# The same instructions on other SBUF addresses: all matmul operands of a two-layer decoder trunk at 128 modulo 512 bytes

## The chip, the cores and the metric

The kernel runs on one core of a Trainium2 chip. The metric is the time of one execution on the device in microseconds; the median of three runs of the kernel before is 2660.34 us (2660.19 to 2660.78). A profile of one further execution is used beside it. A core has TensorE (PE, matrix products, with the weight loads PEld), VectorE (DVE), ScalarE (ACT), GpSimd (POOL) and SyncE (SP, which issues most DMAs). SBUF is the memory that TensorE reads its two operands from: the stationary one, loaded ahead as weights, and the moving one, streamed through. An SBUF tile has 128 partitions and lies at the same byte address in each of them. "At 128" below is short for a byte address that leaves 128 when divided by 512.

## The reference, cut to what matters

Two residual layers over x of 1024 rows and 1024 columns, float32. The first mixes tokens with a gated spatial product in chunks of 128, the second with dilated windowed attention in three patterns; each is followed by a squared-ReLU MLP of width 4096.

```python
for i in range(DEPTH):                       # 2
    shift, scale, gate = ada_mod(c, ada_w[i, 0], ada_b[i, 0])
    h = x * (1.0 + scale) + shift
    y = mixer_a(h, ...) if i % 2 == 0 else mixer_b(h, ...)
    x = layer_norm(ALPHA * x + gate * y, ln_g[i, 0], ln_b[i, 0])
    shift, scale, gate = ada_mod(c, ada_w[i, 1], ada_b[i, 1])
    h = x * (1.0 + scale) + shift
    y = squared_relu_mlp(h, mlp_w_up[i], mlp_w_down[i])
    x = layer_norm(ALPHA * x + gate * y, ln_g[i, 1], ln_b[i, 1])
```

## The kernel before, in words

Nearly all the time goes into matmuls of 128 x 128 weights against 128 x 512 moving columns, in a float32 format of reduced precision. To keep float32 accuracy every operand is cut into a high part (a cast on ScalarE, L113) and a low part (a subtraction on VectorE, L114), and every product takes three matmuls: high by high, high by low, low by high. The names show it: `lhi`, `llo` are the parts of a left operand, `rhi`, `rlo` those of a right one. In a row of the profile `psd<-rhi,lhi` the tile written in PSUM stands first, then the moving operand, then the stationary one.

The stages, in order of time:

- mixer A, about 50 to 330 us: a projection (L530), the spatial product (L415), a second projection (L776), transposes with the identity (L791) and the output projection (L434).
- the MLP of layer 1 (j=1): the up-projection (L989) with seven block products in place of eight, then the down-projection (L1156), again seven products of 192 matmuls each, about 647 to 956 us.
- the projections to q, k and v of attention in blocks (L1500), to about 1330 us.
- attention, about 1375 to 1970 us: for eight pairs of heads and three dilations the scores (L1694, q against k), a softmax, transposes of the probabilities p with the identity (L1747, L1750), the split of the transposed probabilities (`pThi`, `pTlo`), and the product with v (L1774). Between these narrow matmuls of 64 to 256 columns stand the projections of the next q and k (L1601), 512 columns each, three to a step of the contraction, and then the start of the output projection (L1978). The bands of dilation 1 read q and k in blocks from DRAM (`bq`, `bk`).
- the rest of the output projection (L1978), whose weight unit 7 (`wo`) stands in a buffer of the tag `v`, and the MLP of layer 2 (j=3): L989 to about 2340 us, L1156 from about 2350 us to the end.

The modulation vectors (`ada`) are formed in the background: weights are summed by VectorE, split into `adahi` and `adalo`, and summed over partitions by two matmuls against `ones_r` (L161, L162), twenty times in all.

Where a tile lies is decided by pools. A pool takes the next free bytes when it is opened, on the left side upwards, on the right side downwards from the top, and holds one region for each tag. `cst` (constants) and `small` (statistics) stand first on the left; so their sizes shift all that follows. `edge` is a tile on the right that nothing reads: its size alone shifts all pools on the right side. `lead` and `pad` are such tiles on the left.

The order of instructions is written out by hand or kept by the recording layer, engine by engine; a tile's address has no part in it.

The down-projection uses, for its split operands, fourteen places in turn (`split_tile`, L1083): eight in `wts` and six in the pool `split1` or `split3` that the phase opens. In layer 2 that pool stands 128 bytes further than in layer 1, since the statistics of the last row tile (`st4`, L339) take 128 bytes in the pool below it.

Of the kernel before, what the change touches and what calls it, by code (L numbers as in the profile page):

```python
# [10 lines left out]
F32 = mybir.dt.float32  # L11
F32R = mybir.dt.float32r
AF = mybir.ActivationFunctionType
ALU = mybir.AluOpType
# [3 lines left out]
P = 128  # L18
# [11 lines left out]
EPS = 1e-5  # L30
# [5 lines left out]
def trunk(ctx: ExitStack, tc: tile.TileContext, x, c, ada_w, ada_b, ln_g, ln_b, a_w_in, a_b_in,  # L36
# [4 lines left out]
    V, A, G, T = nc.vector, nc.scalar, nc.gpsimd, nc.tensor  # L41

    def pool(stack, name, bufs, **kw):
        return stack.enter_context(tc.tile_pool(name=name, bufs=bufs, reuse_waits="tile", **kw))

    cst = pool(ctx, "cst", 1)
    small = pool(ctx, "small", 4)
    small.tile([P, 16], F32, name="pad", bufs=1)
    edge = pool(ctx, "edge", 1, side="right")
    edge.tile([P, 24], F32, name="edge")  # L50
    act = pool(ctx, "act", 4)
    wts = pool(ctx, "wts", 4)
    work = pool(ctx, "work", 2)
# [3 lines left out]
    y_out = out.rearrange("b s d -> (b s) d")  # L57


    eps = cst.tile([P, 1], F32, name="eps")  # L60
    V.memset(eps[:], EPS)
    cst.tile([P, 24], F32, name="lead")
    ident = cst.tile([P, P], F32, name="ident")
    make_identity(nc, ident[:])
    ones_r = cst.tile([P, P], F32R, name="ones_r")
# [5 lines left out]
    cols_b = cols_c[:, KD : KD + 64]  # L71
    silu_c = cst.tile([P, KD], F32, name="silu_c")
    one = cst.tile([P, 1], F32, name="one")
    with ExitStack() as first:
        tmp = pool(first, "tmp", 1)
        ps0 = pool(first, "ps0", 1, space=PSUM)
        rows_c = tmp.tile([P, P], F32, name="rows_c")
        V.memset(rows_c[:], 0.0)
        nc.sync.dma_start(rows_c[0:KD, :], c.rearrange("b (k p) -> (b k) p", p=P))
        ones = tmp.tile([P, P], F32, name="ones")  # L80
        V.memset(ones[:], 1.0)
        V.tensor_copy(ones_r[:], ones[:])
        V.memset(one[:], 1.0)
        ptc = ps0.tile([P, P], F32, name="rows_ct")
        T.transpose(ptc[:], rows_c[:], ident[:])
        V.tensor_copy(cols_c[:, 0:KD], ptc[:, 0:KD])
        sg = tmp.tile([P, KD], F32, name="sg")
        A.activation(sg[:], cols_c[:, 0:KD], AF.Sigmoid)
        V.tensor_tensor(silu_c[:], cols_c[:, 0:KD], sg[:], op=ALU.mult)

    def g_col(j):
        return cols[:, o_g + j * KD : o_g + (j + 1) * KD]

    def b_col(j):
        return cols[:, o_b + j * KD : o_b + (j + 1) * KD]
# [7 lines left out]
    def bank(kind, name):  # L103
        return ps[kind].tile([P, HALF], F32, name=name, tag=kind)
# [6 lines left out]
    def split(hi, lo, src, hi_engine=A, lo_engine=V):  # L111

        first = A.copy(hi, src) if hi_engine is A else hi_engine.tensor_copy(hi, src)  # L113
        return first, lo_engine.tensor_tensor(lo, src, hi, op=ALU.subtract)  # L114


    ada = [dict() for _ in range(4)]
# [4 lines left out]
    def ada_steps(j, order, raw_bufs=2):  # L122


        i, s = divmod(j, 2)
        todo = []
        for part, h in order:
            box = {}
            w0 = part * D + h * HALF

            def step(k, part=part, h=h, box=box, w0=w0):
                nm = f"{j}_{part}_{h}"
                raw = ada_p.tile([P, HALF], F32, name=f"adaw_{nm}_{k}", tag="adaw", bufs=raw_bufs)
                nc.sync.dma_start(raw[:], ada_w[i, s, k * P : (k + 1) * P, w0 : w0 + HALF])
                if k == 0:
                    acc = box["acc"] = ada_p.tile([P, HALF], F32, name=f"adaacc_{nm}", tag=f"adaacc{part % 2}")
                    ins = V.tensor_scalar(acc[:], raw[:], silu_c[:, 0:1], None, ALU.mult)
                else:
                    acc = box["acc"]
                    ins = V.scalar_tensor_tensor(acc[:], raw[:], silu_c[:, k : k + 1], acc[:], ALU.mult, ALU.add)  # L140
                tc.keep_in_program_order(ins)

            def bias_row(part=part, h=h, box=box, w0=w0):
                if part == 2:
                    row = box["row"] = ada_p.tile([P, HALF], F32, name=f"adab_{j}_{h}", tag="adaw", bufs=raw_bufs)
                    nc.sync.dma_start(row[0:1, :], ada_b[i, s, w0 : w0 + HALF].unsqueeze(0))

            def reduce(part=part, h=h, box=box):
                nm = f"{j}_{part}_{h}"
                acc = box["acc"]  # L150
                hi, lo = (ada_p.tile([P, HALF], F32R, name=f"ada{m}_{nm}", tag=f"ada{m}") for m in ("hi", "lo"))
                if part == 2:
                    V.tensor_tensor(acc[0:1, :], acc[0:1, :], box["row"][0:1, :], op=ALU.add)
                split(hi[:], lo[:], acc[:])
                box["sum"] = (hi, lo)

            def total(part=part, h=h, box=box, w0=w0):
                nm = f"{j}_{part}_{h}"
                hi, lo = box["sum"]
                pst = bank("tr", f"psa_{nm}")  # L160
                T.matmul(pst[:], ones_r[:], hi[:], start=True, stop=False)  # L161
                T.matmul(pst[:], ones_r[:], lo[:], start=False, stop=True)  # L162
                row = ada_p.tile([P, HALF], F32, name=f"gaterow_{nm}", tag="gaterow")
                if part == 2:
                    V.tensor_scalar(row[:], pst[:], 1.0, None, ALU.add)
                    nc.sync.dma_start(gate_dram[j, w0 - 2 * D : w0 - 2 * D + HALF].unsqueeze(0), row[0:1, :])
                    return
                A.copy(row[:], pst[:])
                nc.sync.dma_start(mod_dram[j, part, h * HALF : (h + 1) * HALF].unsqueeze(0), row[0:1, :])

            def fetch(part=part, h=h):
                if part < 2:
                    ada[j][part, h] = cst.tile([P, 4], F32, name=f"ada_{j}_{part}_{h}")
                    nc.sync.dma_start(ada[j][part, h][:], mod_dram[j, part, h * HALF : (h + 1) * HALF].rearrange("(k p) -> p k", p=P))

            def columns(part=part, h=h):
                if part == 2:
                    return
                bias = cols_b[:, 16 * j + 8 * part + 4 * h : 16 * j + 8 * part + 4 * h + 4]
                res = ada[j][part, h][:]  # L180
                V.scalar_tensor_tensor(res, res, float(part), bias, ALU.add, ALU.add)
                if part == 0:
                    sh, sc = ada[j][0, h], ada[j][1, h]
                    mul = cst.tile([P, 4], F32, name=f"mul_{j}_{h}")
                    add = cst.tile([P, 4], F32, name=f"add_{j}_{h}")
                    o = slice(4 * h, 4 * h + 4)
                    V.tensor_tensor(mul[:], g_col(j - 1)[:, o], sc[:], op=ALU.mult)
                    V.tensor_tensor(add[:], b_col(j - 1)[:, o], sc[:], op=ALU.mult)
                    V.tensor_tensor(add[:], add[:], sh[:], op=ALU.add)
                    ada[j]["mul", h], ada[j]["add", h] = mul, add  # L190

            steps = [lambda k=k, step=step: step(k) for k in range(KD)]
            todo.append((steps[:-1] + [bias_row, steps[-1], reduce] if part == 2 else steps + [reduce], (total, fetch, columns)))
        return todo

# [91 lines left out]
    class Residual:  # L287
# [48 lines left out]

        def stats_in_quarters(self, i, quarters):
            if i not in self.st:
                self.st[i] = vec.tile([P, 32], F32, name=f"st_{self.j}_{i}", tag="st4")[:, 0:24].rearrange("p (q n) -> p q n", n=6)  # L339
            for q in quarters:  # L340
                V.bn_stats(self.st[i][:, q, :], self.acc[i][:, q * 256 : (q + 1) * 256])

# [1172 lines left out]
    def attention(form):  # L1515
# [5 lines left out]
        with ExitStack() as ph:  # L1521
            open_psum(ph, "B", sc=2, pv=2, mm=2, tr=2)
            ql = pool(ph, "attn_qlo", 1)
            vec = pool(ph, "vecB", 1)
            qk = {g: pool(ph, f"attn_qk{g}", 1, side="right") for g in (1, 2)}
            qp = pool(ph, "attn", 2)

            near = ql.tile([P, 2 * P], F32, name="near")
            G.iota(near[:], pattern=[[-1, 2 * P]], base=P, channel_multiplier=1, allow_small_or_imprecise_dtypes=True)
# [491 lines left out]
            lead, credit = 7 * KD, 0  # L2021
# [27 lines left out]
    ahead = values_ahead(right)  # L2049
    done = mlp(1, done, ahead)  # L2050
    done, go_on = attention(values(done, right, ahead))
    with ExitStack() as ph:
        open_psum(ph, "C", mm=8)
# [27 lines left out]
```

## Time and profile before

| | |
|---|---|
| median of 3 runs | 2660.34 us |
| the profiled execution | 2658.99 us |
| its span | 2657.3 us |
| instructions in the span | 36921 |
| matmuls on TensorE | 13144 |
| HBM read and written | 365.95 MB and 136.95 MB, 189 GB/s over the span |
| DMA queue of SP | 444.22 MB, 52.5% of 16 engines' span |
| L1156, down-projections, high by high | 344.6 us busy, 880 matmuls, mean 392 ns |
| L989, up-projections, `psua` | 363.1 us busy, 1536 matmuls, mean 390 ns |

A row of the view by line gives line, engine, operation, tiles, shapes and count, then busy microseconds and the mean duration of one in ns, then the idle time of the engine just before, with what ended it. The duration of a matmul is counted from its start to its last result; matmuls overlap, so the distance between two starts is shorter than the duration. The view of one line gives the smallest, the median and the largest duration, and the starts of the first and the last.

### The profile page before, as it was taken

To read this page: it belongs to the slowest core of one execution; us is meant where nothing else is said; L and a number is where in the kernel's file an instruction comes from. 1 tells how busy PE (TensorE), PEld (TensorE's weight loads), DVE (VectorE), ACT (ScalarE), POOL (GpSimd) and SP (SyncE) were. 2 spreads that over 40 slices of the span, in tenths; PEclk is the share of its full clock that TensorE was granted. 3 is DMA by queue.
4 is the path that set the end of the run, shared out by engine and by line. 5 is a ranking of instruction groups with operands and counts; after the bars stand their busy time and mean duration, and the time that the engine had idled before them with its cause. 6 is when DMAs were issued, how large, how long until landed. Compare 5 with 4: busy or idle time off the path is not lost.

```text
span 2657.3 us, 36921 instructions
## 1 busy us (share of the span) xinstructions
PE 2636.0 (99%) x13144; PEld 2178.5 (82%) x13144; DVE 1979.1 (74%) x3558; ACT 1397.0 (53%) x2639; POOL 104.8 (4%) x190
## 2 busy tenths in 40 slices
PE   8999999999999999999999999999999999999998
PEld 6888888888888888888888888888888888888887
DVE  6886898886988787655557777777668965677877
ACT  5454576555444554333446666666657655554432
POOL 0000000000000001111110000000010000000000
PEclk9999999999999999999999999999999999999999
DMA  8543367778867546555565554455783654495562
GB/s 298 186 122 117 129 200 238 238 232 286 315 213 248 184 151 231 196 199 198 176 183 159 151 158 133 133 136 157 238 205 118 225 185 147 157 311 186 182 205 81
DMA packets 341554, 505.35 MB, mean 190 GB/s; under 512 B 58092, under 2 KB 175444, under 8 KB 341368
## 3 DMA queue, kind: packets, MB, share of 16 engines
q1 hardware_dynamic: 324936, 444.22, 52.5%
q0 software_dynamic: 16432, 58.76, 6.2%
q8 instruction: 103, 1.69, 0.3%
q14 instruction: 83, 0.68, 0.1%
HBM read 365.95 MB, written 136.95 MB: 189 GB/s over the span
## 4 chain that ended last, share of the span: by engine, by line
PE 94%; DVE 3%; DMA 2%; ACT 1%; issue 0%; SPq 0%; POOL 0%; DVEq 0%; ACTq 0%; POOLq 0%
PE psd L1156 23%; PE psua L989 13%; PE psv L1500 13%; PE psk L1601 7%; PE psq L1601 7%; PE psuc L989 7%; PE psd_wout L434 3%; PE psu L776 3%; PE psub L989 3%; PE pv L1774 3%; PE sc L1694 3%; PE psv L530 3%; PE pT L1747 1%; PE psoa L1978 1%; PE psoe L1978 1%; PE psod L1978 1%
## 5 line engine op out<-in xcount | busy, mean ns | idle before, releaser
L989 PE MATMUL psua<-right,left 128*128 128x512 f32 x1536 | 363.1, 390 | 0.1
L1156 PE MATMUL psd<-rhi,lhi 128*128 128x512 f32 x880 | 344.6, 392 | 0.0
L1156 PE MATMUL psd<-rhi,llo 128*128 128x512 f32 x880 | 343.3, 390 | 0.0
L1156 PE MATMUL psd<-rlo,lhi 128*128 128x512 f32 x880 | 342.3, 389 | 0.0
L989 PEld LDWEIGHTS psua<-right,left 128*128 128x128 f32 x1536 | 287.2, 188 | 61.7 <-DVE right L114 0.6
L1716 ACT ACTIVATE p<-p,stat 128x128 f32<-128x128 f32 (+1 forms) x384 | 168.8, 441 | 96.0 <-DVE stat L1714 94.9
L1156 PEld LDWEIGHTS psd<-rhi,llo 128*128 128x128 f32 x880 | 165.0, 187 | 36.3
L1156 PEld LDWEIGHTS psd<-rhi,lhi 128*128 128x128 f32 x880 | 165.5, 188 | 35.5 <-ACT part L1020 0.9
L1156 PEld LDWEIGHTS psd<-rlo,lhi 128*128 128x128 f32 x880 | 165.2, 188 | 35.1
L989 PE MATMUL psuc<-right,left 128*128 128x512 f32 x768 | 186.7, 390 | 0.0
L989 PEld LDWEIGHTS psuc<-right,left 128*128 128x128 f32 x768 | 143.7, 188 | 30.8 <-DVE right L114 0.6
L114 DVE TENSOR_TENSOR pTlo<-pT,pThi 128x512 fp32r<-128x512 f32 (+1 forms) x160 | 99.2, 620 | 75.9 <-ACT pThi L113 74.8
L114 DVE TENSOR_TENSOR left<-ws,left 128x512 fp32r<-128x512 f32 x128 | 87.8, 687 | 82.4 <-ACT left L113 80.7
L114 DVE TENSOR_TENSOR llo<-lraw,lhi 128x1024 fp32r<-128x1024 f32 x112 | 136.0, 1216 | 2.4 <-ACT lhi L113 2.4
L1601 PE MATMUL psk<-form_L,wqk_hi 128*128 128x512 f32 x384 | 127.0, 412 | 0.0
L1601 PE MATMUL psq<-form_L,wqk_hi 128*128 128x512 f32 x384 | 126.4, 410 | 0.0
L113 ACT CAST lhi<-lraw 128x1024 fp32r<-128x1024 f32 x112 | 117.0, 1047 | 11.4 <-PE psd L1156 6.8
L1500 PE MATMUL psv<-vrhi,form_S 128*128 128x512 f32 x384 | 119.8, 390 | 1.4 <-DVE vpart L1466 0.9
L113 ACT CAST left<-ws 128x512 fp32r<-128x512 f32 x128 | 79.2, 620 | 78.3 <-DVE ws L913 68.1
L113 ACT CAST pThi<-pT 128x512 fp32r<-128x512 f32 (+1 forms) x160 | 84.8, 530 | 60.9 <-PE pT L1747 44.1
L1714 DVE CUSTOM_DVE_ANT_0 p<-sc,bias 128x128 f32<-128x128 f32 (+1 forms) x384 | 113.4, 345 | 4.4 <-PE sc L1694 4.2
L113 ACT CAST rhi<-rraw 128x1024 fp32r<-128x1024 f32 x48 | 50.4, 1050 | 112.6 <-issue 65.2
(369 smaller groups left out, 6129.2 us busy)
## 6 DMA issues: line engine op xcount, KB each, us to landing
lraw<-forms SPq DMA_DIRECT2D x112, 512.0 KB
adaw<-in_ada_w_dram SPq DMA_DIRECT2D x160, 256.0 KB
up<-in_mlp_w_up_dram SPq DMA_DIRECT2D x64, 512.0 KB
forms<-s SPq DMA_DIRECT2D x128, 256.0 KB
rraw<-in_mlp_w_down_dram SPq DMA_DIRECT2D x64, 512.0 KB
forms<-part SPq DMA_DIRECT2D x96, 256.0 KB
v<-vs POOLq DMA_DIRECT2D x48, 512.0 KB, 3.7
vraw<-in_b_w_qkv_dram SPq DMA_DIRECT2D x42, 512.0 KB
```

What stands on the lines that cost most here:

```text
L113: first = A.copy(hi, src) if hi_engine is A else hi_engine.tensor_copy(hi, src)
L114: return first, lo_engine.tensor_tensor(lo, src, hi, op=ALU.subtract)
L434: T.matmul(p[:], stat[a][:, k, o : o + P], u[b][:, w], start=n == 0, stop=n == count - 1)
L530: ins = T.matmul(sums[i][:], hT[half][a_][:, k, o : o + P], units[c, k // 2][b_][:, n : n + HALF], start=k + a_ + b_ == 0, stop=k == KD - ...
L776: T.matmul(p[:], wu[a_][:, k * P : (k + 1) * P], hT[half][b_][:, k, :], start=k + a_ + b_ == 0, stop=k == KD - 1 and a_ == 1)
L989: T.matmul(acc, w[:, a, k, :], right[p][:, b, k, :], start=p in (1, 2, 5) and k + a + b == 0, stop=k == 3 and a == 1, skip_group_check=True)
L1156: ins = T.matmul(sums[kind, m][:, w], l[a][:, k, m * P : (m + 1) * P], r[b][:, k, w], start=p in (1, 5, 2, 3) and kp + k + a + b == 0 or b ...
L1500: T.matmul(acc, rows[:, m * P : (m + 1) * P], cols_, start=p in (1, 2, 5) and kp + k + a + b == 0, stop=kp == 1 and k == 1 and a == 1, ski ...
L1601: T.matmul(p[:], wu[a][:, k * P : (k + 1) * P], h_op(k, half, b), start=k + c_ == 0, stop=k == KD - 1 and c_ == 2)
L1694: T.matmul(banks[e][:, sl], q_[a][rows, tq], k_[b][rows, keys], start=c_ == 0, stop=c_ == 2)
L1714: V.tensor_tensor_reduce(out=pr, in0=banks[e][:, sl], in1=st["bias"][:, width - w :], scale=-0.125, scalar=3e38, op0=ALU.add, op1=ALU.min, ...
L1716: A.activation(pr, pr, AF.Exp, bias=nm, scale=-1.0, accum_out=l)
```

## The change

No instruction is added, taken out or moved: on each of the five engines the two programs have the same rows in the same order, and the same number of waits. What changes is the size of tiles that stand below others: `pad` (64 bytes) goes, `lead` leaves `cst` and comes back with 128 bytes in the pool of attention, `eps` moves behind the other constants, the modulation columns of three layers share buffers by a tag, `mul` and `add` become two halves of one tile, `st4` moves into `small`, and `edge` grows from 96 to 352 bytes.

```diff
-    small.tile([P, 16], F32, name="pad", bufs=1)
     edge = pool(ctx, "edge", 1, side="right")
-    edge.tile([P, 24], F32, name="edge")
+    edge.tile([P, 88], F32, name="edge")
...
-    eps = cst.tile([P, 1], F32, name="eps")
-    V.memset(eps[:], EPS)
-    cst.tile([P, 24], F32, name="lead")
     ident = cst.tile([P, P], F32, name="ident")
...
     one = cst.tile([P, 1], F32, name="one")
+    eps = cst.tile([P, 1], F32, name="eps")
+    V.memset(eps[:], EPS)
...
-                    ada[j][part, h] = cst.tile([P, 4], F32, name=f"ada_{j}_{part}_{h}")
+                    ada[j][part, h] = cst.tile([P, 4], F32, name=f"ada_{j}_{part}_{h}", tag=f"ada_{part}_{h}")
...
-                    mul = cst.tile([P, 4], F32, name=f"mul_{j}_{h}")
-                    add = cst.tile([P, 4], F32, name=f"add_{j}_{h}")
+                    both = cst.tile([P, 8], F32, name=f"mul_add_{j}_{h}")
+                    mul, add = both[:, 0:4], both[:, 4:8]
...
-                self.st[i] = vec.tile([P, 32], F32, name=f"st_{self.j}_{i}", tag="st4")[:, 0:24].rearrange("p (q n) -> p q n", n=6)
+                self.st[i] = small.tile([P, 4, 6], F32, name=f"st_{self.j}_{i}", tag="st4", bufs=1)
...
             qp = pool(ph, "attn", 2)
+            qp.tile([P, 32], F32, name="lead", bufs=1)
```

What the pools make of it, by the byte addresses of the tiles in the two programs, modulo 512:

| tiles | before | after |
|---|---|---|
| `ident`, `ones_r`, `cols` | 256 | 128 |
| v, `pTlo`, `bias`, `bq`, `bk`, and the `wo` of unit 7 | 0 | 128 |
| q and k (`qhi`, `qlo`, `khi`, `klo`), the residual rows `acc`, `adahi`, `adalo`, `adaw` | 384 | 128 |
| the six tiles of `split3` (j=3: part of `lhi`, `llo`, `rhi`, `rlo`) | 256 | 128 |
| `stat` (three buffers) | 128, 256, 384 | 256, 384, 0 |
| hT, `right`, `left`, `form`, `wqk`, `pThi`, p, `vr`, `winv`, `winu`, `wout`, `split1` and the other `wo` | 128 | 128 |

A slice of an operand starts a multiple of 512 bytes into its tile, so each has its tile's residue. The program has 13128 matmuls. Before, 9316 have both operands at 128, 1876 have both at another residue, the same for the two, and 1936 have operands of different residues. After, 13104 have both at 128; the 24 left are eight transposes of `stat` and the sixteen one-column sums of L610.

More of the change, by code (lines that the diff above doesn't have):

```diff
@@ L183, in columns @@
                     sh, sc = ada[j][0, h], ada[j][1, h]
-                    mul = cst.tile([P, 4], F32, name=f"mul_{j}_{h}")
-                    add = cst.tile([P, 4], F32, name=f"add_{j}_{h}")
+                    both = cst.tile([P, 8], F32, name=f"mul_add_{j}_{h}")
+                    mul, add = both[:, 0:4], both[:, 4:8]
                     o = slice(4 * h, 4 * h + 4)
-                    V.tensor_tensor(mul[:], g_col(j - 1)[:, o], sc[:], op=ALU.mult)
-                    V.tensor_tensor(add[:], b_col(j - 1)[:, o], sc[:], op=ALU.mult)
-                    V.tensor_tensor(add[:], add[:], sh[:], op=ALU.add)
+                    V.tensor_tensor(mul, g_col(j - 1)[:, o], sc[:], op=ALU.mult)
+                    V.tensor_tensor(add, b_col(j - 1)[:, o], sc[:], op=ALU.mult)
+                    V.tensor_tensor(add, add, sh[:], op=ALU.add)
                     ada[j]["mul", h], ada[j]["add", h] = mul, add
```

## The prediction

> **What bounds the kernel now.** I read the page first: busy shares, the slices, the chain. Then the waits of TensorE alone, because the chain says that nothing else matters, and then single lines of it, stage by stage.
>
> ```profile
> span 2657.3 us, 36921 instructions
> PE 2636.0 (99%) x13144; PEld 2178.5 (82%) x13144; DVE 1979.1 (74%) x3558; ACT 1397.0 (53%) x2639; POOL 104.8 (4%) x190
> PEclk9999999999999999999999999999999999999999
> PE 94%; DVE 3%; DMA 2%; ACT 1%; issue 0%; SPq 0%; POOL 0%; DVEq 0%; ACTq 0%; POOLq 0%
> ```
>
> TensorE is busy for 99% of the span at the full granted clock, and 94% of the chain is its work. A busy engine might still hide waits, so the second view is what TensorE waited for (microseconds in total, times, longest):
>
> ```profile
> PE rows_ct L85 <- DMA rows_c<-in_c_dram: 4.7, 1, 4.7
> PE warm L591 <- ACT hT L628: 4.5, 1, 4.5
> PE psv L1500 <- DVE vpart L1466: 0.9, 2, 0.6
> ...
> PE psv L530 <- ACT hT L252: 0.2, 1, 0.2
> ```
>
> The whole list has eight rows and 12.3 us, and 9.2 of these lie before the first real product. So from the first product on, the time is the sum of the distances between starts of matmuls. An edit can help only by making these distances shorter, and a faster or slower VectorE, ScalarE or DMA changes nothing as long as it stays under this cover.
>
> **The change part by part.** It removes and adds no instruction, moves none on any engine, and adds no wait: the two programs have the same rows and the same number of waits on all five engines. The new shared tags of the ada columns put three layers in one buffer, but a column is last read where mul and add are formed, a layer before the next fetch. So the edits of `cst`, `small` and `st4` cost nothing themselves; what they do is shift addresses, and the only question is what an address is worth to a matmul. The trace has an experiment on this in it. The down-projection runs twice, with the same code (L1156), the same 192 matmuls to a product, and the same three terms. In the first (j=1) every operand lies at 128 modulo 512. In the second (j=3) the six tiles of the pool `split3` lie at 256. Here are 160 us of each: instruction, count, duration min/median/max in ns, first and last start, shapes.
>
> ```profile
> 700.00:860.00 160.00, 160.00 (x708) 132.40 (x707) 133.88 (x147) 70.08 (x80) 10.81 (x20) 1.00 0.70 237
> 2400.00:2560.00 160.00, 160.00 (x699) 130.86 (x698) 127.40 (x132) 65.17 (x69) 0.00 (x0) 1.00 0.55 176
> ...
> L1156 PE MATMUL psd<-rhi,lhi x236: 387/389/389, 699.7 to 859.5; 128*128 128x512 f32 x118
> L1156 PE MATMUL psd<-rlo,lhi x236: 389/389/395, 699.9 to 859.7; 128*128 128x512 f32 x118
> ...
> L1156 PE MATMUL psd<-rhi,lhi x233: 389/393/398, 2399.7 to 2559.4; 128*128 128x512 f32 x117
> L1156 PE MATMUL psd<-rlo,lhi x233: 388/388/398, 2399.9 to 2559.7; 128*128 128x512 f32 x117
> L1156 PE MATMUL psd<-rhi,llo x233: 388/391/404, 2400.1 to 2559.9; 128*128 128x512 f32 x117
> ```
>
> Both windows are full, at clock 1.00, and the first has the busier VectorE, ScalarE and DMA, yet it holds nine matmuls more. By the first and last start, 236 triples span 159.8 us: 159.8/235 is 680 ns a triple, 226.7 ns a matmul. In the second, 159.7/232 is 688 ns, 229.5 ns. The medians show where: 389 in every term where all is at 128, up to 393 where one operand is 128 bytes away from the other.
>
> Term one, then: the second down-projection has 7 x 192 + 12 = 1356 matmuls (the last row tile's final pieces come in halves), and after the change its operands lie as those of the first. 1356 x 2.8 ns = **3.8 us**. No cover is involved, since TensorE waits for nobody in either window, and the busier first window shows that the feeders keep up at the faster pace.
>
> Terms two and three are the same effect at two smaller places.
>
> ```profile
> L161 PE MATMUL psa<-adahi,ones_r x12: 404/404/404, 394.2 to 2132.2; 128*128 128x512 f32 x12
> L162 PE MATMUL psa<-adalo,ones_r x12: 402/402/402, 394.4 to 2132.5; 128*128 128x512 f32 x12
> L1978 PE MATMUL psod<-wo_hi,oTs x48: 389/389/389, 1981.0 to 1997.1; 128*128 128x512 f32 x48
> ...
> L1978 PE MATMUL psod<-wo,oTs x24: 387/394/398, 1997.3 to 2002.7; 128*128 128x512 f32 x24
> ```
>
> The sums of the modulation (L161, L162) read ada halves at 384 against ones at 256: 15 and 13 ns over 389, for 20 matmuls each, 40 x 14 = **0.6 us**. Weight unit 7 of the output projection (`wo`) stands in a `v` buffer at 0 against rows at 128: 5 ns over its neighbours `wo_hi`, which do the same work a moment before; 48 x 5 = **0.2 us**. The sums also stand singly in the stream of L989, whose 2688 matmuls have a mean of 390 and a median of 389:
>
> ```profile
> L989 PE MATMUL psua<-right,left 128*128 128x512 f32 x1536 | 363.1, 390 | 0.1
> ```
>
> If the whole nanosecond were their after-effect, 2.7 us would go; if none, nothing. The median says that nearly all the stream is undisturbed, so I take a small part, **0.4 us**.
>
> Term four is attention, and here the trace of before has no row of the new layout. v, the low parts and the banded blocks move from 0, q and k from 384, the identity from 256; the projection of q and k (L1601), which fills the gaps between them, is at 128 already.
>
> ```profile
> L1601 PE MATMUL psq<-form_L,wqk_hi x48: 389/389/389, 1331.9 to 1364.1; 128*128 128x512 f32 x48
> ...
> L1601 PE MATMUL psq<-form_L,wqk_lo x168: 387/393/398, 1377.6 to 1890.1; 128*128 128x512 f32 x168
> L1601 PE MATMUL psk<-form_L,wqk_hi x343: 387/395/505, 1374.7 to 1906.9; 128*128 128x512 f32 x172
> ...
> L1747 PE MATMUL pT<-ident,p 128*128 128x128 f32 x384 | 82.0, 272 | 0.0
> L1774 PE MATMUL pv<-pTlo,v 128*128 128x128 f32 x240 | 58.4, 274 | 0.0
> L1774 PE MATMUL pv<-pThi,v 128*128 128x128 f32 x240 | 52.1, 247 | 0.0
> L1774 PE MATMUL pv<-pThi,v 128*128 128x256 f32 x160 | 44.6, 287 | 0.4 <-ACT pThi L113 0.2
> L1774 PE MATMUL pv<-pTlo,v 128*128 128x256 f32 x160 | 44.1, 285 | 0.8 <-DVE pTlo L114 0.7
> ```
>
> Before attention begins, the same line runs at 389 flat; between small matmuls its median is 393 to 395, though its own operands agree. Either the other residues of the small ones disturb it, or any small matmul does. If it is all the residues, 1536 matmuls x 5 ns = 7.7 us go; if none, nothing. It can also lose, which the rivals price. What row is nearest? The small ones show hardly any trace of residue: 256 columns take 287 ns where the operands differ (pThi at 128, v at 0) and 285 where they agree (both 0). So I stand near the lower end and take **1.0 us**.
>
> The sum is 3.8 + 0.6 + 0.2 + 0.4 + 1.0 = **6.0 us** of gain. The profiled execution took 2658.99 us (span 2657.3) and should come to 2653.0 (span 2651.3). The median of the three runs, 2660.34, is 1.35 above it; from that, **2654.3**.
>
> A rule of the Trainium skill speaks against the change. The page "TensorE: Matmul & The Clock Gate", section "Step-by-step: what each phase is for", says that TensorE has two independent ports into SBUF, so that loading the next weights takes nothing from the running matmul. By that rule alone residues could not matter and the sum would be nothing, 2660.3; the two windows of L1156 above disagree by 2.8 ns a matmul, so the rule gets the small chance of the second rival.
>
> **The rivals.**
>
> First, attention settles wholly: L1601 falls to 389 and the 7.7 us go instead of 1.0. Then the time is 2660.3 - 5.0 - 7.7 = 2647.6. For it: its operands agree already, so something around it disturbs it. Against it: the pv rows, where agreement bought nothing. 17%, with whatever lies down to 2651.
>
> Second, the address is not the cause. j=3 also multiplies by a gate on VectorE and stores other results, and the nine matmuls might be due to that; or the shift doesn't arrive at the operands. Then the time is 2660.3. Against it: TensorE waits for nobody there, `wo` beside `wo_hi` is the same difference in another stage, and all operands but those of 24 matmuls do come to lie at 128. 8%.
>
> Third, the change ends slower: equal residues collide in the narrow matmuls of attention. At 128 columns pTlo, which agrees with v at 0, takes 274 ns and pThi, which differs, 247. If agreement is what makes the one slow, 240 x 27 = 6.5 us are added, and 560 transposes that go from 272 to 274 add 1.1. With 5.0 us gained elsewhere that is 2660.3 - 5.0 + 7.6 = 2662.9. It decides from a loss of 5.0/240 = 21 ns a pThi. Against it: the two take turns, hi always first, and the order explains the row as well. In time (start, duration, count at the end):
>
> ```profile
> 1651.03 0.28 PE L1774 MATMUL pv<-pThi,v 128*128 128x256 f32 x1
> 1651.14 0.28 PE L1774 MATMUL pv<-pTlo,v 128*128 128x256 f32 x1
> 1651.27 0.22 PE L1774 MATMUL pv<-pThi,v 128*128 128x128 f32 x1
> 1651.33 0.27 PE L1774 MATMUL pv<-pTlo,v 128*128 128x128 f32 x1
> ```
>
> The short one is the 128-column pThi that follows a wide one, whose streaming has covered its weight load. With its smaller forms, where attention loses a part of what the rest gains, 17%.
>
> **How the numbers follow.** The forecast and its own range of 2651 to 2657 have 58%, the first rival 17%, the second 8%, the third 17%. A difference of 0.2%, 5.3 us, is about what a measurement of this kernel can tell from no change, so faster means under 2655.0, and the forecast stands only 0.7 us inside. I give six tenths of its own chance to that side, 35%, and with the first rival 52%. The rest is within 0.2%, but for 4% in which the third rival is twice as dear. The range holds 8 in 10 when it takes in the forecast's own, most of the first rival and the milder half of the third: 2649 to 2659.
>
> **What would show it.** Right: L1156 at 389/389 in all three terms between 2395 and 2610 us and 944 starts in 214 us; L161 and L162 near 389; `psod<-wo` at 389; still no waits on TensorE. Term four is read from L1601: a median of 393 to 395 says no gain, 389 the first rival. The third rival would show in pThi at 128 columns near 274. Wrong would be a new row in TensorE's waits, or L1156 unchanged at 393.

## The result, and the profile after

| | before | after |
|---|---|---|
| median of 17 runs each, us | 2660.68 (2659.07 to 2661.77) | 2655.63 (2654.06 to 2659.16) |
| ratio, 95% interval | | 0.9983 [0.9975, 0.9990] |
| the profiled execution, us | 2658.99 | 2655.62 |
| its span, us | 2657.3 | 2653.9 |

The change makes the kernel 5.05 us faster. The forecast was a gain of 6.0 us, to 2654.3. The measured time lies 0.6 us above 2655.0, the line under which the prediction had put 52%. One kernel told of below (`attention_at_0`) had two of its twelve runs at a mean granted clock of 0.902 and 0.565, the profiled one among them, so that only the times of the other ten are used. The page of after, first the span, the engines' busy time, the granted clock by slices, and the shares of the chain:

```profile
span 2653.9 us, 36921 instructions
PE 2631.0 (99%) x13144; PEld 2179.2 (82%) x13144; DVE 1979.9 (75%) x3558; ACT 1397.1 (53%) x2639; POOL 104.8 (4%) x190
PEclk9999999999999999999999999999999999999999
PE 70%; issue 21%; DVE 4%; POOL 2%; DMA 1%; ACT 1%; POOLq 0%; SPq 0%; DVEq 0%; ACTq 0%
```

Counts and clock are those of before, and TensorE is still busy for 99%. The chain seems to tell another story, 70% PE in place of 94%. It does not: at one wait of 1.0 us in L1600 it turns from TensorE to VectorE, and then follows other engines and transfers from about 1340 us back to about 680 us, a stretch in which TensorE was busy all the same. So the waits of TensorE are read beside it (line and tile, what it waited for, microseconds in total, times, longest):

```profile
PE warm L589 <- ACT hT L626: 5.3, 1, 5.3
PE rows_ct L83 <- DMA rows_c<-in_c_dram: 4.5, 1, 4.5
PE psk L1600 <- DVE qlo L112: 1.0, 1, 1.0
PE psv L1498 <- DVE vpart L1464: 0.9, 2, 0.6
PE pv L1773 <- DVE pTlo L112: 0.7, 2, 0.4
...
PE pst L893 <- ACT h L897: 0.2, 1, 0.2
```

9.8 us of the total of 13.7 us lie before the first real product, as 9.2 of 12.3 did. The third row and the last one are new. (Line numbers of after are one or two smaller: L1600 is L1601 of before, L1154 is L1156.)

Then the two down-projections. Of the two windows' rows the columns are the window, its length, the busy time of PE, PEld, DVE, ACT and POOL with their counts, the clock, the DMA's share and GB/s. The rows of the line are from the second down-projection.

```profile
700.00:860.00 160.00, 160.00 (x708) 132.47 (x707) 135.09 (x148) 70.72 (x80) 11.21 (x21) 1.00 0.72 239
2400.00:2560.00 160.00, 160.00 (x707) 132.48 (x707) 128.34 (x134) 67.27 (x71) 0.00 (x0) 1.00 0.55 176
...
L1154 PE MATMUL psd<-rlo,lhi x236: 388/390/394, 2389.6 to 2549.4; 128*128 128x512 f32 x118
L1154 PE MATMUL psd<-rhi,llo x236: 388/389/397, 2389.8 to 2549.7; 128*128 128x512 f32 x118
L1154 PE MATMUL psd<-rhi,lhi x236: 387/390/390, 2390.1 to 2549.9; 128*128 128x512 f32 x118
```

The second window holds 707 matmuls where it held 699, one fewer than the first, and (2549.4 - 2389.6) / 235 / 3 is 226.7 ns from start to start in place of 229.5. Next the two smaller places, the sums of the modulation and weight unit 7:

```profile
L159 PE MATMUL psa<-adahi,ones_r x12: 389/390/390, 394.2 to 2132.9; 128*128 128x512 f32 x12
L160 PE MATMUL psa<-adalo,ones_r x12: 389/390/390, 394.4 to 2133.2; 128*128 128x512 f32 x12
...
L1977 PE MATMUL psod<-wo,oTs x24: 389/389/390, 1998.2 to 2003.4; 128*128 128x512 f32 x24
```

404, 402 and 394 have all come to 389 or 390. Last, attention, where the medians of the projection and the means of the product with v are read:

```profile
L1600 PE MATMUL psq<-form_L,wqk_lo x161: 387/393/402, 1385.4 to 1891.0; 128*128 128x512 f32 x161
L1600 PE MATMUL psk<-form_L,wqk_hi x325: 386/396/506, 1394.7 to 1899.8; 128*128 128x512 f32 x163
...
L1773 PE MATMUL pv<-pTlo,v 128*128 128x128 f32 x240 | 58.7, 277 | 0.1
L1773 PE MATMUL pv<-pThi,v 128*128 128x128 f32 x240 | 52.0, 247 | 0.0
L1773 PE MATMUL pv<-pThi,v 128*128 128x256 f32 x160 | 44.4, 286 | 0.3 <-ACT pThi L111 0.2
```

Nothing moved: 393 and 396 against 393 and 395, and 247 and 286 against 247 and 287.

The starts of each stage's first matmul cut the span into stages; the last row ends with the last matmul. On this scale mixer A runs from 20 to 322 us, and the first down-projection from 636 to 945 us, 11 us earlier than the list of stages has it. The last column is an experiment told below, the change with one part undone.

| stage, us | before | after | edge_undone |
|---|---|---|---|
| up to the first matmul of L530 | 19.99 | 20.60 | 19.78 |
| mixer A: L530, L776, L434 | 301.83 | 301.24 | 301.04 |
| up-projection j=1 | 314.31 | 313.55 | 313.59 |
| down-projection j=1 | 308.95 | 308.85 | 308.87 |
| block projections (L1500) | 386.89 | 387.24 | 387.26 |
| first q and k, up to the first scores | 38.17 | 39.42 | 38.90 |
| attention | 539.87 | 539.95 | 540.19 |
| output projection, up to psod | 71.04 | 71.02 | 71.01 |
| psod | 21.91 | 21.76 | 21.76 |
| psoe, up to j=3 | 25.82 | 25.93 | 25.93 |
| up-projection j=3 | 310.70 | 310.56 | 310.57 |
| down-projection j=3 | 309.23 | 305.28 | 305.28 |

The spans differ by 3.4 us only, the medians by 5.05. Two rows hold this. The start is 0.61 us later, in the first waits for data. And the stage of the first q and k is 1.25 us longer, with the new wait of 1.0 us in it. VectorE's waits between 1330 and 1385 us, before and after, show what stood behind that:

```profile
DVE qs L114 <- ACT qs L113: 5.0, 3, 3.5
```

```profile
DVE qs L112 <- ACT qs L111: 6.5, 3, 4.7
```

The split of q came late by 1.2 us in this execution. It doesn't go with the layout: of the kernels below that have the new layout or nearly so, some have no such wait (38.17 us with everything at 192), some a part of it (0.4 us in edge_undone), and one with only a part of the change has 0.2. That it is scatter is read from these few profiles; no run was made for it alone. The block projections are 0.35 us longer, but they take 387.26 us also in the kernel below that changes nothing before the second down-projection; so a few tenths of a microsecond in a stage can be scatter as well.

### The profile page after: what moved, and what is told of

Read it like the earlier page. It is cut to its first block, busy times and chain, and to the rows that moved or that the text cites. A ratio compares the mean times of both kernels' runs of the same rounds, so it can differ in the third digit from the quotient of the medians.

```text
span 2653.9 us, 36921 instructions
## 1 busy us (share of the span) xinstructions
PE 2631.0 (99%) x13144; PEld 2179.2 (82%) x13144; DVE 1979.9 (75%) x3558; ACT 1397.1 (53%) x2639; POOL 104.8 (4%) x190
## 4 chain that ended last, share of the span: by engine, by line
PE 70%; issue 21%; DVE 4%; POOL 2%; DMA 1%; ACT 1%; POOLq 0%; SPq 0%; DVEq 0%; ACTq 0%
PE psua L987 13%; PE psd L1154 12%; PE psk L1600 7%; PE psuc L987 7%; PE psq L1600 6%; PE psd_wout L432 3%; PE psub L987 3%; PE psv L528 3%; PE pv L1773 3%; PE psu L774 3%; PE sc L1693 3%; PE pT L1746 1%; POOL v L1475 1%; PE psoa L1977 1%; POOL qk L1470 1%
## 5 line engine op out<-in xcount | busy, mean ns | idle before, releaser
L1154 PE MATMUL psd<-rhi,lhi 128*128 128x512 f32 x880 | 343.3, 390 | 0.0
L1154 PE MATMUL psd<-rhi,llo 128*128 128x512 f32 x880 | 342.5, 389 | 0.0
L1154 PE MATMUL psd<-rlo,lhi 128*128 128x512 f32 x880 | 342.4, 389 | 0.0
L1154 PEld LDWEIGHTS psd<-rhi,lhi 128*128 128x128 f32 x880 | 165.3, 188 | 34.8 <-ACT part L1018 0.9
L1154 PEld LDWEIGHTS psd<-rhi,llo 128*128 128x128 f32 x880 | 165.3, 188 | 34.2
L1154 PEld LDWEIGHTS psd<-rlo,lhi 128*128 128x128 f32 x880 | 165.3, 188 | 33.8
L1600 PE MATMUL psk<-form_L,wqk_hi 128*128 128x512 f32 x384 | 127.3, 413 | 1.0 <-DVE qlo L112 1.0
L1600 PE MATMUL psq<-form_L,wqk_hi 128*128 128x512 f32 x384 | 126.7, 411 | 0.0
L138 DVE SCALAR_TENSOR_TENSOR adaacc<-adaw,silu_c,adaacc 128x512 f32<-128x512 f32 x140 | 104.5, 747 | 6.6 <-DMA adaw<-in_ada_w_dram 5.6
```

Of the source, the lines that this page charges most:

```text
L1154: ins = T.matmul(sums[kind, m][:, w], l[a][:, k, m * P : (m + 1) * P], r[b][:, k, w], start=p in (1, 5, 2, 3) and kp + k + a + b == 0 or b ...
L1600: T.matmul(p[:], wu[a][:, k * P : (k + 1) * P], h_op(k, half, b), start=k + c_ == 0, stop=k == KD - 1 and c_ == 2)
```

## The experiments

The theory after the result: a wide matmul is slower if its moving and its stationary operand lie at different addresses, by a certain modulus. Rivals: that 128 itself is a good address; that only a change of distance from one matmul to the next costs; and, for attention, that the narrow matmuls' own addresses matter after all.

### One part alone: the six tiles of the second down-projection

Before, with the statistics tile in the pool below `split3` grown to 512 bytes, so that only these six tiles come to 128.

```diff
-                self.st[i] = vec.tile([P, 32], F32, name=f"st_{self.j}_{i}", tag="st4")[:, 0:24].rearrange("p (q n) -> p q n", n=6)
+                self.st[i] = vec.tile([P, 128], F32, name=f"st_{self.j}_{i}", tag="st4")[:, 0:24].rearrange("p (q n) -> p q n", n=6)
```

> The kernel before with one edit: the pool split3 of the second down-projection comes to lie at 128, all else stays where it was. Theory (the distance of the two operands modulo 512 sets the pace of an unbroken stream): the second down-projection runs at 226.7 ns from start to start like the first, 3.9 us are gained and the time is about 2656.7, ratio 0.9985; the sums of the modulation stay at 404 and 402 ns, attention stays as it was. Rival (the second down-projection is slower for another reason, its gate or its stores): it stays at 229.5 ns and the time at 2660.

Measured: 2656.2 us (2654.92 to 2657.86, 11 runs) against 2659.99 of before beside it, ratio 0.9986 [0.9978, 0.9995], 3.8 us of gain. Two lines of its trace, a down-projection's term and a sum of the modulation:

```profile
L1156 PE MATMUL psd<-rhi,lhi x236: 389/389/395, 2389.8 to 2549.6; 128*128 128x512 f32 x118
L161 PE MATMUL psa<-adahi,ones_r x12: 404/404/404, 395.1 to 2134.0; 128*128 128x512 f32 x12
```

The first has come to 389, the second is still at 404, and the time is down by term one alone. The down-projection j=3 takes 305.28 us, the up-projection j=1 314.33 as before, and attention 539.72. This undoes the second rival of the prediction: gate and stores of j=3 are untouched here, and the matmuls' pace changed with six addresses.

### Parts undone: attention, and the right side

Two kernels start from after. In the first, `v`, the low parts, the bias and the banded blocks go back to 0 (no `lead` in the pool of attention). In the second all that lies on the right side, q, k, `acc` and the ada tiles among it, goes back to 384.

```diff
-            qp.tile([P, 32], F32, name="lead", bufs=1)
```

```diff
-    edge.tile([P, 88], F32, name="edge")
+    edge.tile([P, 24], F32, name="edge")
```

> The kernel after with one edit undone: v, the low parts, the bias and the banded blocks of attention lie at 0 again; q, k and the identity stay at 128. Theory (only unbroken streams of 512 columns feel the distance, narrow matmuls do not): attention takes the same 540 us from the first score to the first output product within 0.3 us, and the whole loses only the 0.2 us of weight unit 7, whose median goes back to 394. Rival (the residues of the narrow matmuls disturb L1600 between them): attention becomes 1 us or more longer, or shorter if equal residues collide there.

> The kernel after with one edit undone: the right side lies at 384 again, with q, k, the residual rows and the ada halves; ones_r and the identity stay at 128. Theory: the two modulation sums stand 256 bytes apart in place of 128, so they are longer than 389 ns, and with the streams after them the up-projection of layer 1 (314.4 us before, 313.6 after) loses up to 0.8 us again; q and k agree with each other, so attention does not move. If a distance of 256 costs nothing, the sums stay at 389 and nothing is lost. The whole: within 1 us of after.

Measured: 2654.6 us (ten runs), ratio 0.9980 [0.9971, 0.9989], and 2654.96 us (2653.62 to 2657.67), ratio 0.9981 [0.9972, 0.9989], both against the same 2659.99. Neither loses any of the gain. And attention as it lies in before took 539.72 us in the kernel with `split3` alone, against 539.95 in after. So the part of the change that is in attention is worth nothing that these runs can tell.

The second has a finding in it. The ada halves lie at 384 again, 256 bytes from `ones_r` at 128:

```profile
L159 PE MATMUL psa<-adahi,ones_r x12: 389/389/389, 393.2 to 2131.7; 128*128 128x512 f32 x12
```

389, where 384 against 256 took 404. Addresses need not agree modulo 512; here modulo 256 is enough.

### Everything at 192

After with 64 bytes more below the identity on the left and 64 less on the right: the 13104 matmuls that had both operands at 128 have both at 192.

```diff
-    edge.tile([P, 88], F32, name="edge")
+    edge.tile([P, 72], F32, name="edge")
...
+    cst.tile([P, 16], F32, name="shift")
     ident = cst.tile([P, P], F32, name="ident")
```

> The kernel after with all its operands moved on by 64 bytes, to 192 modulo 512. Theory (only the distance counts): the time and each stage as after, down-projections at 226.7 ns. Rival (128 modulo 512, or a multiple of 128, is a good address by itself): every stream is slower, by some nanoseconds on each of 10,000 matmuls, so by 20 us or more.

Measured: 2654.63 us (2653.49 to 2656.2, 10 runs), ratio 0.9980 [0.9971, 0.9989].

```profile
L1155 PE MATMUL psd<-rhi,lhi x236: 389/389/395, 2389.7 to 2549.5; 128*128 128x512 f32 x118
```

The same medians, and the same stages to 0.2 us in all wide streams. There is nothing in 128 itself.

### A constant distance of 32, 64, 128 and 256 bytes

After with the pool `wts` shifted by 32, 64, 128 or 256 bytes and the next pool brought back, so that in most products one operand lies that far from the other, always by the same amount. The tile p has one buffer less, to make room. Here for 32:

```diff
+    pool(ctx, "gap1", 1).tile([P, 8], F32, name="gap1")
     wts = pool(ctx, "wts", 4)
+    pool(ctx, "gap2", 1).tile([P, 120], F32, name="gap2")
...
-                                 whole = ql.tile([P, 2 * P], F32, name=f"p_{2 * hp + e}_{g}_{t}", tag="p", bufs=16)
+                                 whole = ql.tile([P, 2 * P], F32, name=f"p_{2 * hp + e}_{g}_{t}", tag="p", bufs=15)
```

> The kernel after with the pool wts moved by 32 bytes against act and all others (p has 15 buffers in place of 16, which makes room): in L987, L774, L1498 and L1600 the two operands stand 32 bytes apart throughout. Theory A (what costs is a distance that is no multiple of 256 bytes): all these streams lie between 226.7 and 233 ns from start to start, some of them clearly over 227. Theory B (what costs is a change of the distance from one matmul to the next; a constant one is absorbed once): 227 ns, and time is lost only where streams of two kinds meet.

> The same by 64 bytes. Theory A: 228 to 233 ns in L987 and L1498, whose 4368 matmuls then cost 6 to 27 us more. Theory B: 227 ns.

> The same by 128 bytes, the distance of the second down-projection and of the modulation sums before. Theory A: the dearest case, 232 to 240 ns in L987 and L1498, 23 to 58 us more on 4368 matmuls. Theory B: 227 ns inside the streams, a few us in all, lost where they meet others.

> The same by 256 bytes. Both theories: no cost, 226.7 ns, the modulation sums with ada at 384 and ones at 128 having shown that for single matmuls. If 512 is the period and those were an exception, 230 ns or more.

Measured, one run each, with 2661.15 for before on the same chip: 2706.7, 2702.25, 2693.08 and 2655.55 us. The same 100 us of the up-projection (L989, j=1) in the four kernels, in this order, by the window's view for this line alone (after the length the busy time of PE and PEld with their counts, the clock, the DMA's share and GB/s):

```profile
400.00:500.00 100.00, 98.78 (x422) 79.03 (x421) 1.00 0.72 233
```

```profile
400.00:500.00 100.00, 99.10 (x425) 79.34 (x424) 1.00 0.71 229
```

```profile
400.00:500.00 100.00, 98.81 (x424) 79.42 (x423) 1.00 0.73 234
```

```profile
400.00:500.00 100.00, 98.84 (x435) 81.28 (x434) 1.00 0.73 235
```

422 to 425 matmuls at 32, 64 and 128 bytes, 435 at 256; 435 is also what after has. All at clock 1.00, and as busy. The busy share, 99 of 100 us in each, doesn't show the loss; only the count does. The durations show a part of it, here for 32, 64, 128 and 256:

```profile
L989 PE MATMUL psua<-right,left x242: 392/395/397, 399.7 to 499.8; 128*128 128x512 f32 x121
```

```profile
L989 PE MATMUL psua<-right,left x240: 392/394/398, 402.0 to 498.3; 128*128 128x512 f32 x120
```

```profile
L989 PE MATMUL psua<-right,left x244: 390/393/404, 399.6 to 499.9; 128*128 128x512 f32 x122
```

```profile
L989 PE MATMUL psua<-right,left x255: 389/389/389, 399.8 to 500.0; 128*128 128x512 f32 x128
```

The block projections answer whether the sign matters, since there `form_S` is the stationary operand in one group and the moving one in another. Of the kernel with 32:

```profile
L1500 PE MATMUL psv<-vrhi,form_S x155: 393/396/397, 1072.1 to 1159.6; 128*128 128x512 f32 x155
L1500 PE MATMUL psv<-form_S,vrhi x96: 395/396/396, 1240.1 to 1284.4; 128*128 128x512 f32 x96
```

396 either way. So the distance costs all along a stream, constant or not, in both directions, unless it is a multiple of 256 bytes among those tried. The kernel with 256 has the same edits as the others, the missing buffer of p too, and loses nothing, so these cost nothing themselves. That 128 would be the dearest was expected wrongly: it is the least dear of the three. The rival that only changes of distance cost has fallen: here the distance stays the same through a stage, and the up-projection j=1 takes 321.83, 321.85 and 320.79 us in place of 313.55.

### Narrow matmuls: v at 64

After with 64 bytes of `lead` in place of 128, so that `v`, the low parts, the bias and the banded blocks lie 64 bytes from the tiles that they meet.

```diff
-            qp.tile([P, 32], F32, name="lead", bufs=1)
+            qp.tile([P, 16], F32, name="lead", bufs=1)
```

> The kernel after with v, the low parts, the bias and the banded blocks of attention at 64 modulo 512, so 64 bytes (no multiple of 256) from pThi, the rows and the identity. Theory (narrow matmuls are bound by their weight load and hide the distance): attention 540.0 us within 0.4, pThi against v at 247 and 286 ns as before; only weight unit 7 loses, 48 matmuls by 5 to 7 ns, 0.3 us. Rival (a distance that costs a wide matmul 7 ns costs a narrow one as much): 400 matmuls of pThi lose 2.8 us.

Measured: 2653.45 us in one run, before 2659.99; attention 539.29 us, the least of all. Its pv rows, and unit 7 of the output projection, which stands in a `v` buffer:

```profile
L1773 PE MATMUL pv<-pThi,v 128*128 128x128 f32 x240 | 52.0, 247 | 0.0
L1773 PE MATMUL pv<-pThi,v 128*128 128x256 f32 x160 | 44.2, 285 | 0.3 <-ACT pThi L111 0.2
...
L1977 PE MATMUL psod<-wo,oTs 128*128 128x512 f32 x24 | 5.8, 394 | 0.0
```

At 64 bytes apart the wide product has gone from 389 to 394, in the same kernel in which the narrow ones stand at 247 and 285 as ever. So these matmuls of 128 and 256 columns show nothing of a distance that 512 columns feel; this rests on one profile.

### Longer runs between the narrow matmuls

If the addresses of the narrow ones don't matter, what lifts L1600 from 389 to 395 in attention? The starts say: after each narrow group the first wide matmuls come too late. The step from one start of L1600 to the next is, over 226.7 ns, on average 5.3 to 6.5 ns longer behind the second to the fourth wide one of a run in after, 1.7 to 3.5 behind the fifth to the seventh, at most 2.6 to the tenth and nothing behind the eleventh. In before these are the same to about 0.8 ns. (The step behind the first is left out: it is some 73 ns longer in both, since the first starts early behind a narrow one.) Most runs between narrow groups are three or six long, so nearly all of L1600 lies in this tail. Two kernels issue the same stream in pieces of two and of four steps in place of one, for fewer breaks. Here for four:

```diff
-            lead, credit = 7 * KD, 0
+            lead, credit = 7 * KD, 1053
...
-                    while credit >= 351:
-                        credit -= 351
-                        next(stream, None)
+                    while credit >= 1404:
+                        credit -= 1404
+                        for _ in range(4):
+                            next(stream, None)
```

> The kernel after with one change of order: the projections of q and k are drawn two steps at a time, so L1600 comes in runs of 6 matmuls and more between the narrow ones, in place of 3 and more; nothing else. Theory (any narrow matmul, whatever its address, leaves the stream after it out of step for some six matmuls): fewer breaks, so the mean excess of L1600 over 226.7 ns falls from 3.9 ns to about 3, and attention is 1 to 2 us shorter, if no wait appears. Rival (the other engines' traffic in attention disturbs it): the excess stays at 3.9 ns.

> The same with four steps at a time, runs of 12 matmuls and more. Theory: the excess of L1600 falls to 2 ns or less, its median duration to 389 to 391, attention 2 to 4 us shorter, unless the narrow matmuls now come late and TensorE waits. Rival: the median stays at 393 to 395.

Measured: 2657.49 us (2655.17 to 2659.47), ratio 0.9991 [0.9982, 1.0], and 2663.26 us (2662.39 to 2664.54), ratio 1.0013 [1.0004, 1.0023], both against 2659.99 of before. The time was missed: no gain over after with two, and a loss with four. The excess moved the right way, from 4.3 ns a step in after to 4.0 and 3.0, less than hoped. Two of L1600's rows with runs of four:

```profile
L1600 PE MATMUL psk<-form_L,wqk_hi x313: 387/390/793, 1393.1 to 1900.0; 128*128 128x512 f32 x157
L1600 PE MATMUL psq<-form_L,wqk_lo x160: 387/393/397, 1390.0 to 1898.3; 128*128 128x512 f32 x160
```

The median of the first fell from 396 to 390, yet attention takes 549.88 us in place of 539.95. The windows of after and of runs of four (columns as in the down-projections), and new waits of TensorE in the latter:

```profile
1385.00:1900.00 515.00, 514.67 (x3488) 433.63 (x3487) 367.11 (x1118) 328.41 (x975) 19.79 (x46) 1.00 0.54 148
```

```profile
1385.00:1900.00 515.00, 507.53 (x3417) 429.18 (x3415) 359.89 (x1110) 325.06 (x970) 20.26 (x46) 0.99 0.53 145
```

```profile
PE sc L1693 <- DVE stat L1713: 2.6, 1, 2.6
PE pv L1773 <- DVE pTlo L112: 2.3, 6, 0.5
PE pv L1773 <- ACT pThi L111: 2.2, 3, 1.3
```

TensorE is idle for 7.5 us of the 515 in place of 0.3: it waits for VectorE and ScalarE, which the fine order had covered. The clock of 0.99 is a second loss. Shortly behind a wait of 1.3 us, and again behind the one of 2.6 us, the granted clock falls to a half for 3.4 us; no other stretch between the first and the last products of this profile, and none of after's, has less than the full clock. The first of the two, in the same columns:

```profile
1449.50:1452.90 3.40, 3.40 (x10) 2.63 (x9) 0.38 (x1) 0.00 (x0) 0.00 (x0) 0.50 0.08 5
```

Some 1400 matmuls x 1.3 ns, 1.8 us, were to be had. Attention is 9.9 us longer in their place: about 7 for the waits and an estimated 3.4 for the clock (half of twice 3.4 us), less the 1.8, which leaves about a microsecond open. That the waits bring the clock down is read from these two places alone.

## Why the prediction was right, and where a size was off

**What bounds the kernel** held. TensorE is busy for 99% before and after, and every gain that the stages show is a shorter distance between starts. The waits after the first real product changed by 0.8 us.

**Term one** held: 3.95 us by the stage (309.23 to 305.28) for 3.8, and 3.8 us in the timed runs of the kernel with this part alone. L1154 stands at 389 or 390 in all three terms. The window of 214 us that was to hold 944 starts holds 944 in after, and 932 in before (the view counts 946 and 934, with the two that still run as it begins).

**Terms two and three and the after-effect** held in sum. The modulation's sums fell to 389 or 390. The stages in which they stand lost 0.28 (L776), 0.76 (L989, j=1) and 0.14 us (j=3); the kernel with `split3` alone has none of this. That is 1.2 us for the 0.6 + 0.4 of the text. But the after-effect is the larger share, where the text had it as the smaller one. In the stream of L989 the starts of before around each pair of sums add up to 79 ns more than 226.7 apiece: 27 ns at the pair itself, 5 or 6 at the wide matmul ahead of it and 46 at the nine behind. Sixteen such pairs stand in the three stages, and 16 x 79 ns is 1.26 us. The matmul ahead of a pair is slow although both its own operands are at 128; the weights of L161, `ones_r` at 256, are loaded while it runs. It is the later of the two in the first row below, at 396 ns. The next two rows begin with start and duration in us, and the last row has the same two matmuls in after:

```profile
L989 PE MATMUL psua<-right,left x2: 389/392/396, 393.7 to 393.9; 128*128 128x512 f32 x2
393.92 0.19 PEld L161 LDWEIGHTS psa<-adahi,ones_r 128*128 128x128 f32 x1
394.15 0.40 PE L161 MATMUL psa<-adahi,ones_r 128*128 128x512 f32 x1
L987 PE MATMUL psua<-right,left x2: 390/390/390, 393.8 to 394.0; 128*128 128x512 f32 x2
```

`psod` lost 0.15 us for 0.2. `psoe` shows no gain (25.82 to 25.93, its `wo` rows from 393 to 392): its starts came closer there too (median 232 to 227.5 ns), but a new wait of the transposes behind it, the 0.2 us of `pst` for ScalarE above, takes that back.

**Term four** was the one mis-sized as a whole: 1.0 us, measured nothing (539.87 to 539.95 in the profiles, and no loss in the timed runs with attention put back at 0). The text took "near the lower end"; the lower end itself was right. It left open whether the residues of the small matmuls or any small matmul disturbs L1601. The runs say the second: v at 64 changes nothing, the excess by place behind a narrow matmul is nearly the same in before and after, and only longer runs lower it.

With 3.95 + 1.2 + 0.15 = 5.3 us these stages of the profile come near the 5.05 measured, whose interval by the ratio is 2.7 to 6.7 us. The forecast of 6.0 lies in it; 1.0 of it was term four.

**The rivals.** That attention settles wholly: not so, L1600 kept 393 to 396. That equal residues collide: not so, pThi at 128 columns kept 247 ns with everything at 128, and the order explains its 27 ns less than pTlo. Sorted by what stands ahead of it, pThi takes 274 ns on average behind 128 columns (111 of the 240, in before and after), the same as pTlo, and 221 to 226 behind 256 or 512 columns; the mean of 247 mixes the two. That the address is not the cause: not so, by the down-projection with six tiles moved and by the four distances. The rule of the Trainium skill behind it (page "TensorE: Matmul & The Clock Gate", section "Step-by-step: what each phase is for": a weight load takes nothing from the running matmul) would, as the prediction read it, give no difference between any of these kernels. The traces do not agree: 2706.7, 2702.25 and 2693.08 us against 2655.55 are measured, and the measurement decides. **What would show it wrong** was, in part, a new row in TensorE's waits. There are two. The 1.0 us for qlo hides a part of the gain in this one profile; other kernels of the new layout run without it. The 0.2 us of `pst` stands also in the profiles of `edge_undone`, of everything at 192 and of the distance of 256.

## What to carry to other kernels

In a stream of wide matmuls of this format that TensorE alone bounds, put the moving and the stationary operands of all of them at the same byte address modulo 256. Look for a loss not in the busy share, which is 99% either way, but in the number of matmuls in equal windows, or in a median duration a few nanoseconds above that of the same shape elsewhere. A small tile below a pool, statistics or a row of constants, is enough to shift a whole stage; here narrow matmuls gained nothing from it, nor did the wide ones scattered between them.

## What the runs showed of the hardware

Among the distances tried, the cost goes by the distance modulo 256 bytes: 384 against 128 is free (389 ns), 384 against 256 is not (404). It is larger than before's trace showed: with 64 bytes between the operands of most products the whole kernel takes 46.6 us more, 1.8%. Distances of 32 and 64 bytes are dearer than 128 (51.1 and 46.6 against 37.5 us over after). The same five products of the down-projection j=1, 960 matmuls, take 217.63 us at no distance, 223.57 and 223.37 with `wts` 32 and 64 bytes on, and 220.39 with 128, the very time of the second down-projection in before. In the up-projection j=1, where every product has the distance, its 1344 matmuls lose 6.2 ns each at 32 and 64 bytes and 5.4 at 128 (from 321.83, 321.85 and 320.79 us against 313.55).

A wide stream stays out of step, by 5 to 6 ns a matmul at first, for about ten matmuls behind a narrow one, at all the addresses tried there; behind a pair of sums at a distance it stays so for nine. Whether a matmul feels the distance to its own weights or to the next one's, which are loaded while it runs, is not settled: with a constant distance the two are the same. The slow matmul ahead of each pair, whose own operands agree, speaks for the next one's. Why the period is 256 bytes, and what in the reading of SBUF takes the time, stays open: no run here looks inside a matmul. No kernel tried beats after by more than the runs can tell; the four nearest (edge_undone, everything at 192, attention at 0, v at 64) lie between 2653.45 and 2654.96 us.
